# Second layer's output weights loaded from the sync queue, behind the activations of the first two token blocks

## The chip, the cores and the metric

The kernel runs on one core of one Trainium2 chip. The metric is the device time of the whole kernel in microseconds (us); the kernel before is given as the median of three runs, 2333.69 us (2331.33 to 2339.92). The engines are called as in the profile: PE (matrix products and transposes), DVE (VectorE), ACT (ScalarE), POOL (GpSimd) and SP (SyncE, which here only issues transfers).

## The reference

The reference is an encoder of two layers over 1024 tokens of width 1024. The first layer mixes tokens with latent attention, the second with differential attention; both are block-causal over chunks of 64 tokens and have 8 heads. Each layer is

```python
h = _layernorm(ALPHA * h + mix, ln_mix_g[i], ln_mix_b[i])
h = _layernorm(ALPHA * h + _swiglu(h, ffn_w_gu[i], ffn_w_down[i]), ln_ffn_g[i], ln_ffn_b[i])
```

What the change touches is the end of the second layer's mixer, in which the heads' outputs `o`, normalised per head, go through the output weights `w_o` (8 heads of 128 rows by 1024 columns):

```python
o = _rmsnorm(o, g_sub) * (1.0 - lambda_init)
return o.reshape(b, s, DIFF_HEADS * DIFF_V) @ w_o
```

All is float32.

## The kernel before, in words

Products are made in three passes of a reduced format: each operand is split into a high and a low part (`hi`, `lo`), and high by high, high by low and low by high are added up. The split of an activation is one ACT instruction (the high part) and one DVE instruction (the low part). Tokens are worked on in 8 blocks of 128.

*Attention of the second layer* (lines 1190 to 1371) goes over 8 heads and, in each, over the 8 token blocks; `attention` writes the sequence out. For each block PE makes two sets of scores (`s_b`, line 217), DVE adds the bias and finds the row limits (line 220), ACT takes the exponential (line 223), DVE the reciprocal (line 225), POOL scales one of the two maps (line 1269) and DVE adds the two (line 1270). PE then turns the result around (`pt_b`, line 149), ACT and DVE split it (lines 244 and 245), and PE multiplies it with the values (`o_b`, line 256). Scores run two blocks ahead. Other work is put between the blocks by a table of slots, `fill`, with `at(slot, function)`. In the last head the blocks come in the order of `LAST_ORDER`: 6, 7, 4, 5, 2, 3, 0, 1.

*The output product of the second layer* is begun inside the last head. Its class is `OutProj` (line 326). `begin_out` (line 1357), in slot 54, opens it: it frees the layer's input `xT`, which PE reads last in the projections of the last head (`bp`, lines 144 to 146), and in that room asks for the activations and the weights. Heads 0 to 5 (`HEADS = H - 2`) are complete by then and lie in DRAM; `of(tb)` (line 350) loads them for one token block as 128 rows of 6 pieces of 128 numbers (`of_a`, line 355), splits them (`split`, lines 378 and 379), and loads the residual `z` (line 373). The weights of the eight heads lie in DRAM already split (`wo_dr`): heads 0 to 5 come in one load of 1 MB each (`wo`, line 342), heads 6 and 7 in two loads of 0.5 MB each (`who` and `wlo`, line 347). `early` (line 400) multiplies the first two blocks, 6 and 7, with heads 0 to 5 in slots of the last head (`zp_a`, line 390, from `product`); `late` (line 409) adds heads 6 and 7; `rest` (line 417) does the other six blocks and the layer norm, whose scale and shift it loads into `gb` (line 420, 2 x 0.5 MB).

*What sets the order.* Each engine works through its own list of instructions in a fixed order; one that waits holds up all behind it. The order within a list is made when the kernel is built, by a scheduler that follows priorities and an estimate of when each instruction will be ready; a change of one transfer can thus move other instructions too. Issues of transfers stand in the lists of SP and POOL like any other instruction. Each of the two has eight landing signals for its transfers, used in turn, so that an issue also waits for the landing of the one eight before it on that queue.

Of the kernel before, what the change touches and what calls it, by code (L numbers as in the profile page):

```python
# [38 lines left out]
LAST_ORDER = (6, 7, 4, 5, 2, 3, 0, 1)  # L39
# [3 lines left out]
def trunk(  # L43
# [32 lines left out]
    nc = tc.nc  # L76
# [31 lines left out]
    def f32(t):  # L108
        return t.bitcast(F32)
# [216 lines left out]
    class OutProj:  # L326
# [5 lines left out]
        def __init__(self, side, w_dr, o_dram, o_here, x_src, x_dst, scale):  # L332
            self.st = ExitStack()
            self.pool = self.st.enter_context(tc.tile_pool(name="op1", bufs=2, side=side, reuse_waits="tile"))
            self.o_dram, self.o_here, self.x_src, self.x_dst, self.scale = o_dram, o_here, x_src, x_dst, scale
            self.oh, self.z, self.sums, self.m = {}, {}, {}, {}
            self.of(LAST_ORDER[0])
            self.wo = []
            for h in range(H):
                if h < self.HEADS:  # L340
                    t = self.pool.tile([P, 2, D], F32R, tag=f"wo{h}", name=f"wo1_{h}", bufs=1)
                    nc.gpsimd.dma_start(t, w_dr[h])
                    self.wo.append((t[:, 0], t[:, 1]))
                else:
                    t = [wp.tile([P, D], F32R, tag=f"w{p}", name=f"w{p}o1_{h}") for p in "hl"]
                    for p in range(2):
                        nc.gpsimd.dma_start(t[p], w_dr[h][:, p])
                    self.wo.append(t)

        def of(self, tb):  # L350
# [684 lines left out]
    with ast as st:  # L1035
# [106 lines left out]
        def at(slot, fn, *args):  # L1142
            fill.setdefault(slot, []).append(lambda: fn(*args))
# [47 lines left out]
    with ExitStack() as st:  # L1191
# [162 lines left out]
        first, second = LAST_ORDER[:2]  # L1354
# [7 lines left out]
        at(b, begin_out)  # L1362
        for slot, what, args in (
            (2, "early", (first, (0, 1))), (3, "early", (first, (2, 3))), (4, "early", (first, (4, 5))),
            (4, "of", (second,)), (6, "early", (second, (0, 1, 2))), (7, "early", (second, (3, 4, 5))),
            (9, "late", (first,)),
        ):
            at(b + slot, lambda what, *a: getattr(proj[0], what)(*a), what, *args)
# [97 lines left out]
```

## Time and profile before

| | |
|---|---|
| median of three runs | 2333.69 us |
| the three runs | 2331.33, 2339.92, 2333.69 us |
| the profiled execution, first to last instruction | 2331.5 us |
| instructions | 31115 |
| granted PE clock, mean | 0.991 |
| transfers | 288.29 MB, mean 124 GB/s |
| on SP's queue | 96480 packets, 267.48 MB |
| on POOL's queue | 5856 packets, 18.81 MB |

The profile is one execution, and the page gives no other time of it than the span. Times in its rows count from the first instruction. A row of a timeline has start, duration, engine, line of the kernel, operation, `out<-in` by the program's names and the shape; in brackets stand the idle time ahead and what ended it. A name such as `of_a` is the tile without its buffer number, so `of_a` stands for all eight blocks. The durations of matmuls overlap: a row's duration is longer than its step to the next.

### The profile page before, as it was taken

The numbers are of one execution on the slowest core, as the hardware profiler recorded it, in microseconds if no ns is written. First come the engines' busy times: TensorE is split into PE (matmuls) and PEld (weight loads), VectorE is DVE, ScalarE is ACT, GpSimd is POOL, SyncE is SP. The second block draws the span as 40 slices with busy tenths as digits, with TensorE's granted clock in tenths as the row PEclk, the third lists the DMA queues.
The fourth block names the chain that finished last, engine by engine and source line by source line (L and its number), as shares of the span: only waits on it lengthen the run. The fifth ranks groups of instructions, "written<-read, shape, count | busy, mean of one in ns | idle before, by whom it ended". The sixth has DMA issues, their size and how long they took to land. (4 is left out here: it accounts for less than half of the span.)

```text
span 2331.5 us, 31115 instructions
## 1 busy us (share of the span) xinstructions
PE 2254.7 (97%) x11410; PEld 1918.7 (82%) x11410; DVE 1556.9 (67%) x2876; ACT 1017.4 (44%) x2089; POOL 894.8 (38%) x706
## 2 busy tenths in 40 slices
PE   7899999999999999999999999979999999999997
PEld 7898997888888887888888898867788888887885
DVE  4567664596656667677576666666596656658777
ACT  4366664352333333444465656545342333324353
POOL 3233452014444445555432424222014444436564
PEclk9999999999999999999999999989999999999999
DMA  5112324344323238454220212153334323337353
GB/s 201 35 57 89 120 90 161 109 163 153 118 85 131 73 118 320 172 194 153 91 55 19 69 37 69 37 190 101 124 141 151 107 98 106 111 131 303 142 203 118
DMA packets 102490, 288.29 MB, mean 124 GB/s; under 512 B 7856, under 2 KB 30000, under 8 KB 91840
## 3 DMA queue, kind: packets, MB, share of 16 engines
q1 hardware_dynamic: 96480, 267.48, 32.4%
q0 software_dynamic: 5856, 18.81, 2.5%
q8 instruction: 90, 1.47, 0.3%
q14 instruction: 64, 0.52, 0.1%
HBM read 205.00 MB, written 77.07 MB: 121 GB/s over the span
## 5 line engine op out<-in xcount | busy, mean ns | idle before, releaser
L470 ACT CAST op_g<-gr 128x512 fp32r<-128x512 f32 x240 | 147.5, 622 | 410.7 <-PE gb L515 228.1
L471 POOL TENSOR_TENSOR op_g<-gr,op_g 128x512 fp32r<-128x512 f32 x104 | 145.9, 1408 | 303.0 <-DVE tmp L606 153.6
L471 DVE TENSOR_TENSOR op_h<-rh,op_h 128x512 fp32r<-128x512 f32 x154 | 161.4, 1078 | 69.9 <-ACT op_h L470 69.9
L515 PE MATMUL ga<-xh_m,op_g 128*128 128x512 f32 x512 | 168.0, 389 | 0.0
L470 ACT CAST op_h<-rh 128x512 fp32r<-128x512 f32 x154 | 92.9, 619 | 147.7 <-PE dx L783 37.2
L783 PE MATMUL dw<-op_w_t,op_h 128*128 128x512 f32 x660 | 151.4, 390 | 0.2 <-DVE op_h L471 0.2
L783 PEld LDWEIGHTS dw<-op_w_t,op_h 128*128 128x128 f32 x660 | 123.6, 188 | 26.1 <-DVE op_h L471 0.6
L223 ACT ACTIVATE l_b<-l_b,mx_b 128x256 f32<-128x256 f32 (+7 forms) x128 | 99.6, 778 | 76.0 <-DVE mx_b L220 74.3
L1269 POOL TENSOR_SCALAR l_b<-l_b,r_b,cst 128x128 f32<-128x128 f32 (+3 forms) x64 | 52.8, 825 | 204.0 <-DVE r_b L225 194.8
L471 POOL TENSOR_TENSOR op_w_t<-tt,op_w_t 128x512 fp32r<-128x512 f32 x66 | 98.7, 1499 | 78.7 <-ACT op_w_t L470 76.8
L783 PE MATMUL dx<-op_w_b,op_h 128*128 128x512 f32 x528 | 122.6, 391 | 5.9 <-ACT op_w_b L470 3.9
L783 PEld LDWEIGHTS dx<-op_w_b,op_h 128*128 128x128 f32 x528 | 98.4, 188 | 29.8 <-ACT op_w_b L470 4.7
L515 PE MATMUL gb<-t4h_f,op_g 128*128 128x512 f32 x352 | 115.8, 390 | 3.2 <-DVE tmp L598 3.2
L515 PE MATMUL gc<-b22h_f,op_g 128*128 128x512 f32 x352 | 115.6, 389 | 1.0 <-ACT op_g L470 1.0
L471 DVE TENSOR_TENSOR op_g<-gr,op_g 128x512 fp32r<-128x512 f32 x136 | 109.5, 806 | 9.0 <-ACT op_g L470 8.8
L515 PE MATMUL gc<-t1h_f,op_g 128*128 128x512 f32 x352 | 115.5, 389 | 0.0
L515 PE MATMUL gb<-t3h_f,op_g 128*128 128x512 f32 x352 | 115.2, 389 | 0.0
L515 PE MATMUL gb<-t2h_f,op_g 128*128 128x512 f32 x352 | 114.9, 389 | 0.0
L515 PEld LDWEIGHTS ga<-xh_m,op_g 128*128 128x128 f32 x512 | 96.1, 188 | 20.0
L471 POOL TENSOR_TENSOR op_g<-s,op_g 128x512 fp32r<-128x512 f32 x40 | 55.9, 1398 | 142.9 <-ACT op_g L470 142.9
L144 PE MATMUL bp<-xT_f,h_wb 128*128 128x512 f32 x256 | 103.0, 402 | 0.1
L146 PE MATMUL bp<-xT_f,l_wb 128*128 128x512 f32 x256 | 101.6, 397 | 0.0
(381 smaller groups left out, 6788.5 us busy)
## 6 DMA issues: line engine op xcount, KB each, us to landing
gr<-in_w_gu SPq DMA_DIRECT2D x44, 1024.0 KB, 6.6
rh<-h_dr SPq DMA_DIRECT2D x28, 1024.0 KB, 4.9
h_dr<-sh SPq DMA_DIRECT2D x22, 1024.0 KB, 4.9
h_dr<-hp SPq DMA_DIRECT2D x22, 768.0 KB, 4.1
tt<-in_w_dn SPq DMA_DIRECT2D x22, 512.0 KB, 7.6
rh<-h_dr SPq DMA_DIRECT2D x14, 768.0 KB, 4.4
z<-xs_dr SPq DMA_DIRECT2D x16, 512.0 KB, 10.0
rw_b<-in_w_dn SPq DMA_DIRECT2D x8, 1024.0 KB, 8.8
```

The source lines that it names most:

```text
L144: T.matmul(ps_out, lh, rh, start=(i == 0), stop=False)
L146: T.matmul(ps_out, ll, rh, start=False, stop=(i == n - 1))
L223: A.activation(l[:, :n], l[:, :n], AF.Exp, bias=mx, scale=-1.0, accum_out=sm)
L470: A.copy(hi, src)
L471: eng.tensor_tensor(lo, src, f32(hi), ALU.subtract)
L515: T.matmul(o, w[:, a, kc], x[b][:, k, :], start=(first and k == 0 and (a, b) == (0, 0)), stop=(k == 3 and a == 1), skip_group_check=True,)
L783: T.matmul(o, h[:, a, c], w[:, b_], start=(first and (a, b_) == (0, 0)), stop=(last and a == 1), skip_group_check=True,)
L1269: G.tensor_scalar(l1[:, :n], l1[:, :n], r1, nlam, ALU.mult, ALU.mult)
```

## The change

Three things change. The loads of all eight heads' weights are issued by SP instead of POOL; since a transfer from SP does not convert, the destination is written as plain float32 (`f32(t)`). `of` is called for both first blocks, 6 and 7, when the output product is opened, ahead of the weights; before, block 7's call stood in a slot four blocks later. That slot's entry goes.

```diff
-            self.of(LAST_ORDER[0])
+            for tb in LAST_ORDER[:2]:
+                self.of(tb)
             self.wo = []
             for h in range(H):
                 if h < self.HEADS:
                     t = self.pool.tile([P, 2, D], F32R, tag=f"wo{h}", name=f"wo1_{h}", bufs=1)
-                    nc.gpsimd.dma_start(t, w_dr[h])
+                    nc.sync.dma_start(f32(t), w_dr[h])
                     self.wo.append((t[:, 0], t[:, 1]))
                 else:
                     t = [wp.tile([P, D], F32R, tag=f"w{p}", name=f"w{p}o1_{h}") for p in "hl"]
                     for p in range(2):
-                        nc.gpsimd.dma_start(t[p], w_dr[h][:, p])
+                        nc.sync.dma_start(f32(t[p]), w_dr[h][:, p])
...
-            (4, "of", (second,)), (6, "early", (second, (0, 1, 2))), (7, "early", (second, (3, 4, 5))),
+            (6, "early", (second, (0, 1, 2))), (7, "early", (second, (3, 4, 5))),
```

Up to this place in the program all engines' lists are the same. Lines of the changed kernel are one higher from line 338 on.

SP's list at the start of the output product, before: the last attention outputs are stored, `of_a` is loaded block by block (the first number in the name is the block), and `zy_a` is a residual.

```order
L1309 DMA o_dr_3_89<-bo 128x256
L355 DMA of_a_6_15086<-o_dr_3_89 128x6x128
L355 DMA of_a_7_15420<-o_dr_3_89 128x6x128
L355 DMA of_a_4_15742<-o_dr_2_88 128x6x128
L355 DMA of_a_5_15833<-o_dr_2_88 128x6x128
L373 DMA zy_a_4_15747<-xs_dr_99 128x1024
```

The same place in the changed kernel:

```order
L356 DMA of_a_6_15086<-o_dr_3_89 128x6x128
L356 DMA of_a_7_15095<-o_dr_3_89 128x6x128
L343 DMA wo_0_15103<-wo_dr_90 128x2048
L343 DMA wo_1_15105<-wo_dr_91 128x2048
L343 DMA wo_2_15107<-wo_dr_92 128x2048
L343 DMA wo_3_15109<-wo_dr_93 128x2048
L343 DMA wo_4_15111<-wo_dr_94 128x2048
L343 DMA wo_5_15113<-wo_dr_95 128x2048
L348 DMA who_6_15115<-wo_dr_96 128x1024
L348 DMA who_7_15119<-wo_dr_97 128x1024
L348 DMA wlo_6_15116<-wo_dr_96 128x1024
L348 DMA wlo_7_15120<-wo_dr_97 128x1024
```

In both, blocks 6 and 7 come next to each other; the ten weight loads now stand behind them, and blocks 4 and 5 behind those.

POOL's list, which is the other side of it, as a piece of before (`l_b` is the softmax map that POOL scales, with head-local block number; `gb` holds the norm's scale and shift):

```order
L1269 TENSOR_SCALAR l_b_6_1_14865<-l_b_6_1_14865,r_b_6_1_14878,cst 128x896
L342 DMA wo_0_15095<-wo_dr_90 128x2048
L342 DMA wo_1_15097<-wo_dr_91 128x2048
L342 DMA wo_2_15099<-wo_dr_92 128x2048
L342 DMA wo_3_15101<-wo_dr_93 128x2048
L342 DMA wo_4_15103<-wo_dr_94 128x2048
L342 DMA wo_5_15105<-wo_dr_95 128x2048
L420 DMA gb_15679<-in_ln_mix_g 128x1024
L420 DMA gb_15679<-in_ln_mix_b 128x1024
L347 DMA who_6_15107<-wo_dr_96 128x1024
L347 DMA who_7_15111<-wo_dr_97 128x1024
L1269 TENSOR_SCALAR l_b_7_1_14916<-l_b_7_1_14916,r_b_7_1_14929,cst 128x1024
```

and of the changed kernel:

```order
L1270 TENSOR_SCALAR l_b_6_1_14865<-l_b_6_1_14865,r_b_6_1_14878,cst 128x896
L421 DMA gb_15679<-in_ln_mix_g 128x1024
L421 DMA gb_15679<-in_ln_mix_b 128x1024
L1270 TENSOR_SCALAR l_b_7_1_14916<-l_b_7_1_14916,r_b_7_1_14929,cst 128x1024
L1270 TENSOR_SCALAR l_b_6_1_15040<-l_b_6_1_15040,r_b_6_1_15053,cst 128x896
```

The ten weight loads are gone from POOL; the two loads of `gb` stay, and now stand first in its queue.

PE's list where it first uses the weights, before (`s_b_7` are the scores of block 7 in the last head, `zp_a_6` the output product of block 6, its two halves of columns 0 and 1):

```order
L217 MATMUL s_b_6_1_1_15046<-bk_10161,ql_10164 128x448
L390 MATMUL zp_a_6_0_0_15248<-wo_0_15095,oh_a_6_15088 128x512 x2
L390 MATMUL zp_a_6_0_0_15248<-wo_0_15095,ol_a_6_15089 128x512
L390 MATMUL zp_a_6_1_0_15255<-wo_0_15095,oh_a_6_15088 128x512 x2
L390 MATMUL zp_a_6_1_0_15255<-wo_0_15095,ol_a_6_15089 128x512
L217 MATMUL s_b_7_0_0_15116<-bk_10161,bq_10159 128x512
L217 MATMUL s_b_7_0_0_15116<-bk_10161,ql_10164 128x512
L217 MATMUL s_b_7_0_1_15121<-bk_10161,bq_10159 128x512
L217 MATMUL s_b_7_0_1_15121<-bk_10161,ql_10164 128x512
L390 MATMUL zp_a_6_0_0_15248<-wo_1_15097,oh_a_6_15088 128x512 x2
```

and now:

```order
L217 MATMUL s_b_6_1_1_15046<-bk_10161,ql_10164 128x448
L391 MATMUL zp_a_6_0_0_15256<-wo_0_15103,oh_a_6_15088 128x512 x2
L391 MATMUL zp_a_6_1_0_15263<-wo_0_15103,oh_a_6_15088 128x512 x2
L391 MATMUL zp_a_6_0_0_15256<-wo_0_15103,ol_a_6_15089 128x512
L391 MATMUL zp_a_6_1_0_15263<-wo_0_15103,ol_a_6_15089 128x512
L217 MATMUL s_b_7_0_0_15124<-bk_10161,bq_10159 128x512
L217 MATMUL s_b_7_0_0_15124<-bk_10161,ql_10164 128x512
L149 MATMUL pt_b_7_0_15155<-ident,l_b_7_0_14901 128x128 x4
L217 MATMUL s_b_7_0_1_15129<-bk_10161,bq_10159 128x512
L217 MATMUL s_b_7_0_1_15129<-bk_10161,ql_10164 128x512
L256 MATMUL o_b_3_15173<-pth_b_6_0_15062,bvh_0_13904 128x256
L149 MATMUL pt_b_7_1_15164<-ident,l_b_7_0_14901 128x128 x4
```

The first use of the first weight keeps its place behind the same row; the transposes of head 6's last block (`pt_b_7`) now come before the second weight's first use, which follows directly behind this piece.

## The prediction

> **What bounds the kernel now.** The page comes first. It says that TensorE (PE) is the bound of the whole kernel, so that only what PE loses can be won.
>
> ```profile
> span 2331.5 us, 31115 instructions
> PE 2254.7 (97%) x11410; PEld 1918.7 (82%) x11410; DVE 1556.9 (67%) x2876; ACT 1017.4 (44%) x2089; POOL 894.8 (38%) x706
> ```
>
> PE is busy for 2254.7 of 2331.5 us, which leaves 77 us without work. The second view is the list of waits, for PE alone around the moment at which the output weights are fetched (1531 to 1595 us), and then for all engines from 1500 to 1600 us. Columns: who waited, for whom, us in total, times, longest.
>
> ```profile
> PE s_b L217 <- DVE mx_b L220: 14.4, 1, 14.4
> PE zp_a L390 <- DMA wo<-wo_dr: 0.6, 1, 0.6
> ...
> ACT oh_a L378 <- DMA of_a<-o_dr: 15.0, 1, 15.0
> DVE oh_a L379 <- ACT oh_a L378: 13.8, 1, 13.8
> ```
>
> One wait of 14.4 us stands there: nearly a fifth of all that PE loses. Read upward it is a chain. PE waits for VectorE (DVE), DVE for ScalarE (ACT), and ACT for one transfer, the load of attention outputs into `of_a`. The third view, the timeline of PE, shows the place and a second loss behind it. Columns: start, duration, then engine, line and instruction; the bracket is the idle time before it and what ended it.
>
> ```profile
> 1533.16 0.37 PE L217 MATMUL s_b<-bk,ql 128*128 128x448 f32 x1
> 1534.10 0.70 PE L390 MATMUL zp_a<-wo,oh_a 128*128 128x512 f32 x2 [0.57 <-DMA wo<-wo_dr]
> ...
> 1550.59 0.80 PE L217 MATMUL s_b<-bk,bq 128*128 128x512 f32 x1 [14.40 <-DVE mx_b L220]
> ...
> 1555.85 0.39 PE L390 MATMUL zp_a<-wo,oh_a 128*128 128x512 f32 x1
> ...
> 1580.44 2.90 PE L390 MATMUL zp_a<-wo,oh_a 128*128 128x512 f32 x12
> ```
>
> The windows view (busy us of each engine in a stretch, number of instructions, then the granted PE clock, the DMA share and GB/s) gives the clock there.
>
> ```profile
> 1533.50:1536.20 2.70, 2.12 (x9) 1.42 (x8) 0.83 (x3) 0.00 (x0) 0.54 (x1) 1.00 1.04 396
> 1536.20:1550.60 14.40, 0.01 (x1) 0.01 (x1) 2.44 (x7) 2.88 (x6) 2.85 (x4) 0.59 1.07 407
> 1550.60:1555.80 5.20, 5.20 (x12) 4.12 (x13) 3.62 (x11) 2.38 (x4) 1.08 (x1) 0.50 1.13 386
> 1555.80:1589.30 33.50, 33.50 (x207) 29.41 (x205) 24.88 (x76) 20.18 (x53) 7.78 (x8) 1.00 0.05 15
> 1589.30:1600.00 10.70, 8.82 (x37) 6.69 (x36) 9.13 (x28) 7.20 (x20) 1.98 (x3) 0.85 0.39 123
> ```
>
> PE stands still for 14.40 us, and then runs its next 12 matmuls, from 1550.59 to 1555.85, at half the clock: 5.26 us. The 12 alike at 1580.44 take 2.90 us with the tail of the last; the steps are (2.90 - 0.39) / 11 = 0.228 us, so 12 steps are 2.74 us and the slow clock costs 2.52 us. During the standstill the DMA engines are full (share 1.07, 407 GB/s).
>
> Why that one transfer was late is read from the timelines of SyncE (SP), ACT and POOL, and from the list of DMA issues (last column: us from issue to landing), the first and the second issue of the pair apart.
>
> ```profile
> 1527.63 0.96 SPq L355 DMA_DIRECT2D of_a<-o_dr  x2
> ...
> 1547.17 0.93 ACT L378 ACTIVATE oh_a<-of_a,cst 128x768 fp32r<-128x768 f32 x1 [14.98 <-DMA of_a<-o_dr]
> ...
> 1527.91 3.25 POOL L342 DMA_DIRECT2D wo<-wo_dr  x6 [3.77 <-PE bp L146]
> 1531.15 0.54 POOL L420 DMA_DIRECT2D gb<-in_ln_mix_g  x1
> 1531.68 0.54 POOL L420 DMA_DIRECT2D gb<-in_ln_mix_b  x1
> 1537.86 1.19 POOL L1269 TENSOR_SCALAR l_b<-l_b,r_b,cst 128x1024 f32<-128x1024 f32 x1
> ```
>
> ```profile
> of_a<-o_dr SPq DMA_DIRECT2D x1, 384.0 KB, 3.6
> ...
> of_a<-o_dr SPq DMA_DIRECT2D x1, 384.0 KB, 19.1
> ```
>
> SP issues the loads of blocks 6 and 7 within 0.96 us. The first lands after 3.6 us, the second, of the same size and issued at about 1528.1, only after 19.1, at 1547.2. In between, GpSimd (POOL) has issued six weight loads of 1 MB on its own queue. The packets of the two queues, from 1532 to 1546 us (packets, MB, share of 16 engines):
>
> ```profile
> q0 software_dynamic: 733, 5.35, 94.8%
> q1 hardware_dynamic: 733, 0.38, 12.9%
> ```
>
> 733 packets each. The DMA engines take one packet from POOL's queue and one from SP's in turn; the weights have packets of 7.3 KB on average (5.35 MB / 733), `of_a` of 0.5 KB. A load of 384 KB thus waits behind some 6 MB. ACT's order is fixed, with both blocks' conversions ahead of its next softmax work, and so everything stands.
>
> **The change part by part.** The weights now go through SP's queue, behind both loads of `of_a`. What SP's queue does with two transfers in flight, I read at another place, where a store of 768 KB and a load of 1 MB are issued 0.43 us apart:
>
> ```profile
> 591.52 0.37 SPq L631 DMA_DIRECT2D h_dr<-hp  x1
> 591.95 0.48 SPq L524 DMA_DIRECT2D gr<-in_w_gu  x1
> ```
>
> ```profile
> h_dr<-hp SPq DMA_DIRECT2D x1, 768.0 KB, 4.1
> ...
> gr<-in_w_gu SPq DMA_DIRECT2D x1, 1024.0 KB, 6.5
> ```
>
> The first lands at 595.6, the second at 598.4, 2.8 us later, which is the time of 1 MB at 375 GB/s. They were served one after the other. So block 7's load will be through before any weight moves.
>
> *Removed.* The standstill, 14.40 us, and the slow clock behind it, 2.52 us; also the old wait for the first weight, 0.57 us, which is reckoned anew below. Together 17.5 us, all on PE's path. POOL loses ten issues of about 0.54 us (3.25 / 6) and its waits for free places; its softmax scaling, which ran at 1537.86, can then run when its input is there. That is worth nothing more by itself, since all that waited for it was behind the same standstill.
>
> *Added: the wait for the first weight.* PE is ready for it at 1533.16 + 0.37 = 1533.5. Its landing is a sum over SP's queue. Block 6 lands at 1527.63 + 3.6 = 1531.2, as now. Block 7 follows; the rate of such packets, while hardly any weight moved (1529.5 to 1530.5 us), is this:
>
> ```profile
> q1 hardware_dynamic: 611, 0.31, 103.2%
> q0 software_dynamic: 3, 0.02, 6.1%
> ```
>
> 768 packets (384 KB at 0.5 KB) at 611 per us are 1.3 us: 1532.5. Then 1 MB of weight at 409 GB/s (5.35 + 0.38 MB in 14 us), 2.6 us: 1535.1. This is the lower end: a wait of 1.6 us. The upper end comes from what stays on POOL's queue. The two rows of the normalisation's scale and shift (`gb`, 2 x 0.5 MB) stood behind the weights and now stand first. They wait only for PE's last read of the key tile whose place they take:
>
> ```profile
> 1527.79 0.40 PE L217 MATMUL s_b<-bk,ql 128*128 128x512 f32 x1
> ```
>
> That ends at 1528.2, so they are issued near 1528.5. The weights of before, issued at 1527.91, had 3 packets through by 1530.5, some 2.5 us later; `gb` will hence start moving at about 1531, in turn with block 7's small packets, and its 1 MB, 2.6 us, comes in ahead of the first weight: 1537.7, a wait of 4.2 us. I take 4.0, near that end, since it follows from the row of 733 to 733. For block 7 this means a landing of up to 1535.1, 12 us earlier than now; ACT then waits some 3 us for it, under PE's wait.
>
> The next weights follow every 2.6 us. Between the first use and the second PE has, by the new order, six matmuls of weights and four of scores, 10 x 0.228 us, and eight transposes, which take this:
>
> ```profile
> 1557.53 1.03 PE L149 MATMUL pt_b<-ident,l_b 128*128 128x128 f32 x8
> ```
>
> That is 3.3 us, and some 13 us over the four uses after it, counted in the same way, against 4 x 2.6 = 10.4 for the loads. So no second wait: 0, with 1 us as the end on the other side.
>
> *Added: the clock after that wait.* Shorter standstills are on record, with and without a slow clock behind them:
>
> ```profile
> 1597.02 0.66 PE L149 MATMUL pt_b<-ident,l_b 128*128 128x128 f32 x2 [1.54 <-DVE l_b L1270]
> ...
> 1126.10 1.09 PE L149 MATMUL xTp_f<-ident,y_f 128*128 128x128 f32 x8 [2.14 <-DVE y_f L184]
> ```
>
> ```profile
> 1596.80:1600.10 3.30, 3.08 (x9) 2.54 (x10) 2.04 (x7) 1.78 (x5) 0.00 (x0) 0.50 0.00 0
> 1123.00:1128.00 5.00, 2.78 (x20) 2.22 (x19) 3.25 (x6) 1.14 (x3) 2.16 (x4) 1.00 0.23 96
> ```
>
> 1.54 us of idle (among short waits) were followed by 3.3 us at clock 0.50; 2.14 us were not followed by any. At half clock 3.3 us do the work of 1.7, so the price is 0 to 1.7 us. I take 0.9. The Trainium skill, "TensorE: Matmul & The Clock Gate", section "Part 1: The HAM clock gate", says that the clock falls after an idle window of about 3.4 us, and that windows run free; by a whole idle window a wait of 4 us, lying across two, would mostly cost nothing, and the time would be 2320.2. The row of 1.54 us speaks for a lower threshold than a whole window, and the row of 2.14 us against a fixed one.
>
> *Moved.* Behind the weights on SP stand the loads of blocks 4 and 5; ACT's wait for `of_a` has a count of 1, so nobody waited for them, although they too landed behind the weights, and they keep that place. The z load of block 7 keeps its place in SP's order. In the later order PE takes some matmuls of blocks 4 and 5 earlier; as PE loses only 10.70 - 8.82 = 1.9 us from 1589.3 to 1600, I put 0 there, between -1 and +1.
>
> *Sum.* 17.5 - 4.0 - 0.9 = 12.6 us. The profiled execution would go from 2331.5 to 2318.9 us. Its span lies 2.2 us under the median of the three runs (2331.33, 2333.69, 2339.92), so on that scale the forecast is 2333.7 - 12.6 = 2321.1 us. Behind the place PE is the bound, as the 33.50 of 33.50 us after 1555.8 show, and what PE gains there reaches the end. The forecast's own range: 17.5 - 1.6 = 15.9 won at best (2317.8), 17.5 - 4.2 - 1.7 - 1.0 - 1.0 = 9.6 at worst (2324.1).
>
> **The rivals.** *The softmax chain takes the standstill's place (2326).* With PE's stop gone, DVE has 31.8 us of work (0.83 + 2.44 + 3.62 + 24.88) in the stretch from 1533.5 to 1589.3, and 43.2 us for it where it had 55.8. That is 74%, just what it kept up from 1555.8 to 1589.3 (24.88 of 33.50). For this rival: each softmax block goes PE, DVE, ACT, POOL, DVE, PE, with two blocks of lead. Against it: PE has weight matmuls to put between. If DVE reached only 66%, the stretch would be 48 us, 7.6 us won: 2326.
>
> *The queue makes no difference (2333.7).* All transfers still share the same DMA engines and the bytes are the same. If block 7's load is late in SP's queue as it was in two, ACT stops as long, and nothing changes. The Trainium skill, "DMA: Bandwidth & Descriptors", section "Issuing engines are not separate DMA queues", says that transfers of all engines run on the same 16 DMA engines and interleave, and that issuing from several saves only issue time; read strictly it gives this case. The trace agrees on the sharing (733 to 733), but the pair at 591.5 us, one after the other, speaks against the conclusion. That the loads are not reordered at all is excluded by the new order.
>
> *The other side: SP's queue serves what is in flight in turn (2340).* Then block 7's packets alternate with those of six weights and `gb`, and it lands when nearly all is through: 8 MB of weights, 1 MB of `gb` and 0.8 MB of `of_a` from 1529 at 409 GB/s end at 1553, 6 us later than 1547.2, and the first weight as late: about 2333.7 + 6 = 2340. It decides from the point at which block 7 lands after 1547.2. For it: a list of issues shows the order of issue, not of service. Against it: the same pair at 591.5.
>
> **How the numbers follow.** Forecast 0.73, softmax chain 0.13, no difference 0.08, the other side 0.06. A measurement of this kernel can tell about 0.5% from no change, 11.7 us, so the bound lies at 2322.0, inside the forecast's range: I give two thirds of the forecast to the side below, 0.49. Within 0.5% are the rest of the forecast, 0.24, the chain, 0.13, the case of no difference, 0.08, and 0.04 of the other side: 0.49. Slower by more, 0.02. The range takes in the forecast's own and the chain, and the scatter of the three runs (2.4 us below the median, 6.2 above): 2314 to 2330.
>
> **What would show it.** Right: block 7's load lands by 1535.5; the 14.4 us wait of PE is gone; in its place stands one wait for `wo` of 2 to 4 us; `gb` moves between 1531 and 1536; the clock is at 0.50 for 3.4 us at most; from then to the end the rows of both traces run in parallel. Wrong: ACT still waits over 10 us for `of_a`, or PE waits for later weights, or PE collects many waits of about 1 us for DVE, or the place is won and lost again further on.

## The result, and the profile after

The changed kernel takes 2321.85 us (median of four runs, 2316.95 to 2322.50), the kernel before on the same chip 2332.51 us (median of four). The ratio is 0.9948 (95% interval 0.9933 to 0.9963): 10.7 us less between the medians. Here and below a ratio is worked out from the single runs of both kernels, so it need not be the quotient of the two medians.

The page of the changed kernel (the profiled execution is that of 2316.95 us):

```profile
span 2315.2 us, 31103 instructions
PE 2252.5 (97%) x11410; PEld 1917.9 (83%) x11410; DVE 1554.9 (67%) x2876; ACT 1017.8 (44%) x2089; POOL 889.8 (38%) x696
```

PE has the same 11410 matmuls and 2.2 us less of busy time; nearly all that was won is idle time. Its two longest waits in the stretch that answers to the one shown of before (1525 to 1600 us):

```profile
PE zp_a L391 <- DMA wo<-wo_dr: 3.0, 1, 3.0
PE pt_b L149 <- DVE l_b L1271: 2.2, 1, 2.2
...
```

The wait of 14.4 us is gone, and so is ACT's for `of_a`. In its place stands one wait of 3.0 us for the first weight. The second row is a wait that was there before too (1.54 us, at 1597.02 in the prediction's rows). The issues on SP, and the landings:

```profile
1523.87 0.96 SPq L356 DMA_DIRECT2D of_a<-o_dr  x2
1524.88 2.91 SPq L343 DMA_DIRECT2D wo<-wo_dr  x6
```

```profile
of_a<-o_dr SPq DMA_DIRECT2D x1, 384.0 KB, 3.5
...
of_a<-o_dr SPq DMA_DIRECT2D x1, 384.0 KB, 4.2
...
wo<-wo_dr SPq DMA_DIRECT2D x1, 1024.0 KB, 7.8
gb<-in_ln_mix_g POOLq DMA_DIRECT2D x1, 512.0 KB, 7.1
```

Block 7's load, issued at 1524.3, takes 4.2 us in place of 19.1 and lands at 1528.5. The first weight lands at 1524.88 + 7.8 = 1532.7. PE there, and at two later places, first in the changed kernel and then in the kernel before (heads 6 and 7 of the output product; first matmul of the feed-forward part):

```profile
1532.80 2.05 PE L391 MATMUL zp_a<-wo,oh_a 128*128 128x512 f32 x4 [3.03 <-DMA wo<-wo_dr]
...
1573.06 0.40 PE L391 MATMUL zp_a<-who,oh_a 128*128 128x512 f32 x1
...
1662.90 0.48 PE L516 MATMUL ga<-xh_m,op_gp 128*128 128x512 f32 x1
```

```profile
1589.26 0.48 PE L390 MATMUL zp_a<-who,oh_a 128*128 128x512 f32 x1
...
1677.94 0.48 PE L515 MATMUL ga<-xh_m,op_gp 128*128 128x512 f32 x1
```

Count from the issue of block 6's load, 1523.87 now and 1527.63 before. It is 49.2 us to heads 6 and 7 where it was 61.6: **12.4 us won at the place**. To the feed-forward part it is 139.0 where it was 150.3, 11.3 won; to the end of the span 791.3 where it was 803.9, 12.5 won. The spans themselves differ by 16.3; the other 3.8 us arose ahead of the place, where the lists of all engines are the same, and are scatter of one execution.

The clock, by windows (PE's granted clock is the third number from the end):

```profile
1529.80:1530.80 1.00, 0.00 (x0) 0.00 (x0) 1.00 (x2) 0.35 (x2) 0.00 (x0) 1.00 0.99 414
1530.80:1532.80 2.00, 0.00 (x1) 0.03 (x1) 2.00 (x5) 1.00 (x2) 0.00 (x0) 0.51 1.02 412
1532.80:1537.70 4.90, 4.90 (x14) 3.86 (x14) 2.00 (x8) 0.66 (x4) 0.00 (x0) 0.50 1.00 415
1537.70:1573.00 35.30, 35.24 (x209) 30.52 (x208) 26.68 (x77) 21.55 (x55) 9.14 (x9) 1.00 0.44 175
```

It falls one us into the wait and stays at 0.50 until 1537.7, 4.9 us after PE is at work again: 4.9 / 2 = 2.4 us lost. After that PE is busy for 35.24 of 35.30 us.

### The profile page after: what moved, and what is told of

It is laid out like the page before. It is cut to its first block, busy times and chain, and to the rows that moved or that the text cites. A ratio compares the mean times of both kernels' runs of the same rounds, so it can differ in the third digit from the quotient of the medians.

```text
span 2315.2 us, 31103 instructions
## 1 busy us (share of the span) xinstructions
PE 2252.5 (97%) x11410; PEld 1917.9 (83%) x11410; DVE 1554.9 (67%) x2876; ACT 1017.8 (44%) x2089; POOL 889.8 (38%) x696
## 5 line engine op out<-in xcount | busy, mean ns | idle before, releaser
L784 PEld LDWEIGHTS dw<-op_w_t,op_h 128*128 128x128 f32 x660 | 123.5, 188 | 25.9 <-DVE op_h L472 0.4
## 6 DMA issues: line engine op xcount, KB each, us to landing
z<-xs_dr SPq DMA_DIRECT2D x16, 512.0 KB, 10.7
```

The lines of the kernel that those rows point to most:

```text
L784: T.matmul(o, h[:, a, c], w[:, b_], start=(first and (a, b_) == (0, 0)), stop=(last and a == 1), skip_group_check=True,)
```

## The experiments

The theory on trial, from the prediction: block 7's load was late because two queues take turns packet by packet, and ACT, DVE and PE stood behind it. The main rivals: the gain comes from POOL, rid of ten issues; or from having the weights on SP's queue at all, whatever stands where.

| run | ratio to before (95%) | median, us | block 7's load, issue to landing, us | block 6's issue to the feed-forward part, us |
|---|---|---|---|---|
| before | 1 | 2332.51 | 19.1 | 150.3 |
| the change | 0.9948 (0.9933 to 0.9963) | 2321.85 | 4.2 | 139.0 |
| e1, weights on SP alone | 0.9949 (0.9935 to 0.9964) | 2321.84 | 19.6 | 138.3 |
| e2, both loads early alone | 1.0011 (1.0002 to 1.0020) | 2335.88 | 19.5 | 151.5 |
| e7, rows of 3 KB | 0.9947 (0.9930 to 0.9964) | 2322.67 | 4.5 | 135.7 |
| e3, all on POOL | 0.9945 (0.9933 to 0.9957) | 2321.05 | 4.0 | 137.8 |
| e10, weights on ACT | 0.9974 (0.9964 to 0.9984) | 2327.69 | 15.2 | 146.0 |
| e11, conversion late | 0.9962 (0.9950 to 0.9975) | 2325.01 | 20.6 | 139.2 |
| e12, conversion early | 0.9992 (0.9982 to 1.0003) | 2330.79 | 19.6 | 145.2 |
| e4, `gb` on SP | 0.9944 (0.9932 to 0.9957) | 2322.63 | 4.1 | 136.7 |
| e5, first weight between | 0.9939 (0.9927 to 0.9952) | 2321.52 | 9.9 | 141.3 |
| e6, e4 and e5 | 0.9926 (0.9913 to 0.9938) | 2317.57 | 6.2 | 135.7 |
| e13, e6 and rows of 3 KB | 0.9935 (0.9922 to 0.9949) | 2318.34 | 6.4 | 135.8 |

The last two columns are worked out from the timelines and landings of each run's one profiled execution, as above. The experiments ran on three other chips, each beside the kernel before, whose medians there were 2332.91 us (e1, e2, e3, e7), 2335.64 (e4, e5, e6, e10) and 2332.36 (e11, e12, e13). Across chips compare the ratios, not the medians.

### The two halves of the change (e1, e2)

e1 leaves block 7's load in its old slot (against the changed kernel):

```diff
-            for tb in LAST_ORDER[:2]:
-                self.of(tb)
+            self.of(LAST_ORDER[0])
...
-            (6, "early", (second, (0, 1, 2))), (7, "early", (second, (3, 4, 5))),
+            (4, "of", (second,)), (6, "early", (second, (0, 1, 2))), (7, "early", (second, (3, 4, 5))),
```

> Half of the change: weights on SP's queue, but block 7's load of of_a asked for in its old slot, so that on SP it stands behind six weights of 1 MB and two halves of the seventh and eighth. My theory (one queue serves in order, and what counts is that block 7's load stands ahead of the weights): about 7 MB of weights, 1 MB of gb beside them and 0.4 MB of block 6 go first, 8.4 MB at 409 GB/s is 20.5 us, so block 7 lands some 20 to 22 us after block 6's issue, ACT and PE stand as before (14 to 17 us), and the time is 2331 to 2337 us, no better than before. Rival (the gain comes from POOL, rid of ten issues, or from the weights being on SP's queue at all): standstill gone, about 2322.

Measured: all of the gain, against the expectation. The load itself is late, as expected and more; SP's timeline, the landing of the later one, and ACT's timeline in e1:

```profile
1523.44 0.37 SPq L355 DMA_DIRECT2D of_a<-o_dr  x1
1523.86 2.91 SPq L342 DMA_DIRECT2D wo<-wo_dr  x6
...
1529.74 0.37 SPq L355 DMA_DIRECT2D of_a<-o_dr  x1
```

```profile
of_a<-o_dr SPq DMA_DIRECT2D x1, 384.0 KB, 19.6
```

```profile
1527.06 0.94 ACT L378 ACTIVATE oh_a<-of_a,cst 128x768 fp32r<-128x768 f32 x1
...
1532.26 1.04 ACT L223 ACTIVATE l_b<-l_b,mx_b 128x896 f32<-128x896 f32 x1
...
1548.57 0.83 ACT L223 ACTIVATE l_b<-l_b,mx_b 128x640 f32<-128x640 f32 x1
...
1549.91 0.96 ACT L378 ACTIVATE oh_a<-of_a,cst 128x768 fp32r<-128x768 f32 x1
```

The load lands at 1549.3, as late after its issue as before and 25.9 us after block 6's issue (20 to 22 were expected), and nobody waits: block 7's conversion, directly behind block 6's in the kernel before, now stands behind six exponentials in ACT's list. The scheduler, which gives each instruction its place by an estimate of when it is ready, had put it there; that it did so because it reckoned the load as later is likely and not shown. So my expectation, which took ACT's list as it was, was wrong. The new theory is that a standstill needs two things: the load late, *and* its conversion ahead of softmax work. e11 and e12 below try it.

e2 is the other half: the weights back on POOL, both loads asked for together.

```diff
-                    nc.sync.dma_start(f32(t), w_dr[h])
+                    nc.gpsimd.dma_start(t, w_dr[h])
...
-                        nc.sync.dma_start(f32(t[p]), w_dr[h][:, p])
+                        nc.gpsimd.dma_start(t[p], w_dr[h][:, p])
```

> The other half: both loads of of_a asked for together, weights still on POOL's queue. My theory: the two queues still take turns packet by packet, 768 packets of 0.5 KB beside as many of 7.3 KB, so block 7 lands 17 to 20 us after its issue and the time is that of before, 2330 to 2335 us. Rival (asking early is what helps): block 7 lands within 6 us, about 2322. Rival (POOL): as before too, so this run doesn't tell it apart.

```profile
PE s_b L217 <- DVE mx_b L220: 15.2, 1, 15.2
```

The standstill of before, and the load again at 19.5 us. The median, 2335.88 us, is 0.9 us above the range that I had given. This half changes little: the two loads stood next to each other in SP's list before, too, and were issued within 0.96 us. Asking for both together is worth nothing by itself.

### The load's lateness (e7, e3, e10)

e7 is the kernel before with another layout of the attention outputs in DRAM, so that a load of `of_a` reads longer rows:

```diff
-    o_dr = [[dr.tile([H, P, 256], F32, name=f"o_dr{l}_{g}") for g in range(4)] for l in range(2)]
+    o_dr = [[dr.tile([H, P, 256], F32, name=f"o_dr0_{g}") for g in range(4)],
+            [dr.tile([2, P, H, P], F32, name=f"o_dr1_{g}") for g in range(4)]]
...
-            src = self.o_dram[tb // 2][:n, :, (tb % 2) * P:(tb % 2) * P + P]
-            nc.sync.dma_start(of, src.rearrange("h p q -> p h q"))
+            nc.sync.dma_start(of, self.o_dram[tb // 2][tb % 2][:, :n, :])
...
```

The stores, not shown here, write to the same layout.

> The kernel before, with both queues and all slots as they were; only the DRAM tile of attention outputs of layer 2 is laid out so that a load of of_a reads rows of 3 KB in place of 0.5 KB (its stores write rows of 0.5 KB in place of 1 KB). My theory (queues take turns packet by packet): block 7's load has 128 packets in place of 768, is through after as many packets of weights, 128 x (7.3 + 3) KB = 1.3 MB, 3.3 us, and lands 5 to 8 us after its issue in place of 19.1; standstill gone, 2319 to 2325 us. Rival (share by bytes, or by bandwidth): lands as late as before, 2332. Rival (POOL's issues): POOL is as busy as before, 2332.

```profile
of_a<-o_dr SPq DMA_DIRECT2D x1, 384.0 KB, 4.5
```

```profile
1528.30 0.94 ACT L377 ACTIVATE oh_a<-of_a,cst 128x768 fp32r<-128x768 f32 x1
1529.64 0.94 ACT L377 ACTIVATE oh_a<-of_a,cst 128x768 fp32r<-128x768 f32 x1 [0.40 <-DMA of_a<-o_dr]
```

Block 7's conversion still stands directly behind block 6's, and ACT waits 0.40 us for the load where it waited 14.98. So here it is the load that came sooner, and not the reader that moved. The packets of the two queues of e7 from 1527.6 to 1529.6 us, while block 7's load moved beside the weights:

```profile
q0 software_dynamic: 75, 0.61, 78.7%
q1 hardware_dynamic: 85, 0.21, 29.0%
```

Both queues still move nearly as many packets as each other, but the larger packets let the load through at once: 4.5 us in place of 19.1, with the same bytes, queues and slots. PE's wait of 14.4 us for softmax work is gone and the gain is that of the change. That settles that the lateness came from turns by packets, and it excludes POOL, which issues all that it did before, as the source of the gain. The Trainium skill, "DMA: Bandwidth & Descriptors", section "Queues, rings and completion order", says that each DMA engine goes round its queues by packets; the 733 to 733 of before and these rows agree, though they don't show how many packets one turn has. The Trainium skill, "DMA: Bandwidth & Descriptors", section "Issuing engines are not separate DMA queues", says that transfers interleave whichever engine started them, and that starting them on several engines saves only issue time. Here the queue decides more than that: e2 and the changed kernel have both loads in the same order and differ in the weights' queue alone, and block 7's load takes 19.5 us in the one and 4.2 in the other.

e3 puts the two loads on POOL's queue, ahead of the weights that stay there (the weights' lines as in e2):

```diff
-            nc.sync.dma_start(of, src.rearrange("h p q -> p h q"))
             first = tb in LAST_ORDER[:2]
+            (nc.gpsimd if first else nc.sync).dma_start(of, src.rearrange("h p q -> p h q"))
```

> Weights on POOL's queue as before, and the two loads of of_a on POOL's queue as well, ahead of them. My theory (a queue serves in order, whichever engine issues): block 7 lands ahead of the weights, 5 to 9 us after its issue; the standstill of 14.4 us shrinks to a wait of 4 to 8 us for of_a and the first weight, as POOL's packets start about 2.4 us after the issue; 2321 to 2328 us. Rival (POOL must be rid of issues): POOL has two issues more than before, its scaling comes later still, 2332 us or more. Rival (share by bytes): as before.

```profile
of_a<-o_dr POOLq DMA_DIRECT2D x2, 384.0 KB, 4.0
```

The loads land 4.0 us after their issue, sooner than the 5 to 9 expected, and the time is that of the change, with two issues more on POOL than before. It isn't SP's queue, then, nor POOL's relief, but one queue with the load ahead of the weights. e10 has the weights of heads 0 to 5 on a third queue, ACT's, so that POOL is as free as in the change:

```diff
-                    nc.sync.dma_start(f32(t), w_dr[h])
+                    nc.scalar.dma_start(f32(t), w_dr[h])
```

> The changed kernel, with the first six weights issued on ACT's queue in place of SP's, the two loads of of_a staying on SP. So POOL is rid of the issues as in the changed kernel, but weights and of_a are on two queues as before. My theory (queues take turns packet by packet): block 7 lands late again, 12 us or more after its issue, and as ACT now also pays for six issues, PE stands 10 us or more: 2329 to 2336. Rival (POOL rid of its issues is the gain): block 7's lateness does no harm, or doesn't occur, 2322 plus ACT's six issues of 0.5 us, 2322 to 2325.

```profile
PE zp_a L391 <- ACT oh_a L379: 8.9, 1, 8.9
```

```profile
q10 hardware_dynamic: 234, 1.72, 60.5%
q0 software_dynamic: 234, 0.84, 31.9%
q1 hardware_dynamic: 375, 0.19, 9.1%
```

From 1532 to 1539 us the weights (q10) and `gb` (q0) move packet for packet; SP's small ones (q1) bring 0.19 MB. These are 375 to 234, so among three queues the turns aren't one for one, and why stays open. The load takes 15.2 us, and here block 6's is late as well (ACT waits 10.8 us for it), so PE stands 8.9 us, where I had expected 10 or more. The time came out 1.3 us under the range that I had given. POOL is rid of the issues here, and yet only half of the gain is there (0.9974 to 0.9948). Three of ACT's six issues stand behind that wait and come only at 1540; what ACT's issues cost by themselves can't be told apart from the late loads here.

### The place in ACT's list (e11, e12)

These two cross the second condition with the first. e11 is the kernel before, all transfers untouched; block 7's conversion is ordered behind block 4's exponentials, the place it had in e1:

```diff
+    last_exp = {}
...
-        A.activation(l[:, :n], l[:, :n], AF.Exp, bias=mx, scale=-1.0, accum_out=sm)
+        last_exp[name] = A.activation(l[:, :n], l[:, :n], AF.Exp, bias=mx, scale=-1.0, accum_out=sm)
...
-            self.split(tb, slice(0, n), of)
+            if tb == LAST_ORDER[1]:
+                with tc.issue_after(last_exp["b7_4_1"].ins):
+                    self.split(tb, slice(0, n), of)
+            else:
+                self.split(tb, slice(0, n), of)
```

> The kernel before, with all its transfers on their old queues and in their old order; only block 7's conversion on ACT is ordered behind the exponentials of block 4 in the last head, where the run with the weights alone on SP had it by itself. My theory now (the standstill needs two things: block 7's load late, and its conversion ahead of the next softmax work in ACT's list; taking away either is enough): the load still lands 17 to 20 us after its issue, but nobody waits for it there, the standstill of 14.4 us is gone, 2318 to 2325 us, the same as the changed kernel. Rival (the load's lateness itself, or POOL's ten issues, cost the time): 2330 us or more.

```profile
of_a<-o_dr SPq DMA_DIRECT2D x1, 384.0 KB, 20.6
```

```profile
1549.92 0.83 ACT L225 ACTIVATE l_b<-l_b,mx_b 128x640 f32<-128x640 f32 x1 [0.54 <-DVE mx_b L222]
1550.75 0.92 ACT L384 ACTIVATE oh_a<-of_a,cst 128x768 fp32r<-128x768 f32 x1
```

The load is as late as ever (20.6 us, landed at 1545.0), the conversion starts without a wait, the standstill is gone. At the place it gains what the change gains (139.2 to 139.0); its ratio is a little higher, with intervals that overlap, and its median lies at the upper edge of the range expected. e12 is the opposite: e1's transfers, but the exponentials of block 7 may only follow block 7's conversion. Its edit is against the changed kernel:

```diff
+    gate = []
...
-        A.activation(l[:, :n], l[:, :n], AF.Exp, bias=mx, scale=-1.0, accum_out=sm)
+        if name.startswith("b7_7_"):
+            with tc.issue_after(gate[1].ins):
+                A.activation(l[:, :n], l[:, :n], AF.Exp, bias=mx, scale=-1.0, accum_out=sm)
+        else:
+            A.activation(l[:, :n], l[:, :n], AF.Exp, bias=mx, scale=-1.0, accum_out=sm)
...
-            for tb in LAST_ORDER[:2]:
-                self.of(tb)
+            self.of(LAST_ORDER[0])
...
+            self.of(LAST_ORDER[1])
...
-            A.activation(oh, o, AF.Copy, scale=self.scale)
+            gate.append(A.activation(oh, o, AF.Copy, scale=self.scale))
```

> Weights on SP with block 7's load behind eight of them, as in the run with the weights alone on SP, but the exponentials of block 7 in the last head are ordered behind block 7's conversion in ACT's list. My theory: the load lands 24 to 27 us after block 6's issue, ACT stops for it for some 10 us, and PE, which has weights' products to put between, stands 4 to 12 us: 2325 to 2334 us. Rival (having the weights on SP's queue is enough by itself): 2322.

```profile
PE zp_a L397 <- ACT oh_a L385: 2.9, 1, 2.9
PE zp_a L397 <- DMA wo<-wo_dr: 2.5, 3, 1.6
PE o_b L262 <- ACT pth_b L250: 2.1, 1, 2.1
PE o_b L262 <- DVE ptl_b L251: 1.3, 1, 1.3
...
ACT oh_a L385 <- DMA of_a<-o_dr: 4.5, 1, 4.5
```

ACT waits for the load (4.5 us, less than the 10 expected), PE collects waits behind it, and no gain is left in the time that can be measured (0.9992, with 1 inside the interval), though the weights are on SP's queue and POOL is rid of them. In the profiled execution 5.1 us are still won at the place (145.2 against 150.3, with e1 at 138.3), so the conversion's place undoes somewhat more than half of the gain there. That speaks against the rivals which credit SP's queue or POOL's relief, and completes the square: load late with the conversion high in the list is slow (before, e2, e12); load soon (the change, e3, e7) or conversion low (e1, e11) is fast.

### What is left of the first weight's wait (e4, e5, e6, e13)

e4 moves `gb` to SP, behind the weights; e5 issues the first weight between the two loads; e6 does both; e13 adds e7's layout.

```diff
-                nc.gpsimd.dma_start(gb[:, i], src.partition_broadcast(P))
+                nc.sync.dma_start(gb[:, i], src.partition_broadcast(P))
```

```diff
-            for tb in LAST_ORDER[:2]:
-                self.of(tb)
+            self.of(LAST_ORDER[0])
             self.wo = []
             for h in range(H):
+                if h == 1:
+                    self.of(LAST_ORDER[1])
```

> The changed kernel, with the two loads of gb on SP behind the weights. My theory (the wait for the first weight is stretched by gb, whose 1 MB moves in turn with it): wo_0 lands some 2.4 us earlier, 6 to 6.8 us after block 6's issue in place of 8.8, PE's wait for it goes from 3.0 to 0.5 us or less, the clock of 0.50 behind it (2.3 us lost) goes too: 4 to 5 us won, 2317 to 2318 us. Rival (the wait is block 7's load and the first 1 MB themselves): wait stays near 3, 2321 to 2322.

```profile
PE zp_a L391 <- DMA wo<-wo_dr: 1.2, 1, 1.2
```

```profile
1535.50:1538.90 3.40, 3.35 (x10) 2.64 (x11) 3.40 (x11) 1.40 (x3) 0.00 (x0) 0.59 1.01 429
```

The wait falls to 1.2 us, not to 0.5, and 3.4 us at a clock of 0.59 follow it still. At the place 2.4 us are won in the profiled execution (136.7 against 139.0), but from there to the end it takes longer, and the time is that of the change: 4 to 5 us were expected, and none can be measured. A part of what was given back shows in the last feed-forward part, where PE waits for `z`, first the change and then e4:

```profile
PE dw L784 <- DVE z L800: 2.8, 2, 1.5
```

```profile
PE dw L784 <- DVE z L800: 4.7, 2, 3.2
```

> The changed kernel, with the first weight's load between those of block 6 and block 7. My theory (gb takes its turn with whatever stands first): block 7's 0.4 MB, 1.3 us, goes out of the first weight's way, its wait falls from 3.0 to 1.0 to 1.7 us; block 7 lands 3 to 5 us later, at which ACT waits a little under PE's work; 0 to 3 us won by the clock behind, 2319 to 2322. Rival (block 7's load is the critical one here too): its lateness of 4 us shows at PE as a wait for DVE, 2322 to 2326.

```profile
PE o_b L256 <- ACT pth_b L244: 3.0, 1, 3.0
PE zp_a L392 <- DMA wo<-wo_dr: 0.8, 1, 0.8
```

The wait for the weight falls to 0.8 us, and a wait of 3.0 us for ACT, which waits 5.7 us for block 7's load (9.9 us), takes its place. The mechanism is the rival's; the time, 2321.52 us, is that of the change.

> Both: first weight between the two loads of of_a, and gb on SP behind the weights. My theory: the first weight lands before PE is ready, no wait for it; block 7 lands 2.6 us later than with gb alone moved, still within 8 us of block 6's issue; 4 to 6 us won against the changed kernel, 2316 to 2318. Rival: block 7 late, a wait of PE for DVE in place of that for the weight, 2320 or more.

```profile
PE zp_a L392 <- DMA wo<-wo_dr: 0.5, 2, 0.3
```

Only 0.5 us of waiting for weights are left. e6 has the lowest median, 2317.57 us, and the lowest ratio, 0.9926 against 0.9948 of the change; the intervals overlap a little (0.9913 to 0.9938, 0.9933 to 0.9963), so that it is better than the change is likely and not shown.

> Candidate: the changed kernel with the first weight between the two loads of of_a, gb on SP behind the weights, and of_a in rows of 3 KB. By my theory each load of of_a is through in about 1 us in place of 1.3 (384 KB at 409 GB/s), so block 7 and the second weight come some 0.5 us earlier than with 0.5 KB rows; that is less than the scatter: 2315 to 2319 us, the same as without the layout within the error. A gain of more than 3 us would say that small packets still cost in one queue.

2318.34 us and 135.8 us at the place, as e6: small rows cost nothing more that can be measured once the load shares no queue turn with the weights.

## Why the prediction was right

*Removed, 17.5 us: right.* The standstill, its slow clock and the old wait for the weight are all gone. e7, e11 and e12 show the chain that the prediction read out of the waits.

*The wait for the first weight, 4.0 taken: 3.0.* The step that was mis-sized is that all of `gb` comes in ahead of the weight, in turn with block 7's small packets. `gb` began to move only between 1527.5 and 1528.0, when block 7's load was nearly through. By the landing of that load, at 1528.5, 0.19 MB of `gb` were in; after that the turns were with the weight. The two queues of the changed kernel from 1528.5 to 1532.7:

```profile
q1 hardware_dynamic: 156, 1.15, 66.3%
q0 software_dynamic: 155, 0.57, 33.1%
```

Packet for packet once more, but the weight's packets are twice as large (7.4 KB to 3.7). So 0.57 MB of `gb` came in beside the weight, and with the 0.19 MB before them 0.76 MB in place of all of its 1 MB.

*The clock, 0.9 taken, 1.7 at most: 2.4.* The bound was wrong. It came from one stretch of 3.3 us at half clock; after this wait half clock held for 4.9 us of PE's work. The nearer row was the one behind the 14.40 us, where half clock held for 5.2 us. The sign that was named for it, at most 3.4 us at 0.50, did not come either.

*Later weights, 0: right.* No second wait for `wo` stands in the list. *The later order, 0: right within its bounds.* With the measured sizes the sum is 17.5 - 3.0 - 2.4 = 12.1, and 12.4 were won at the place. Two errors, of 1.0 us and of 1.5 us, nearly cancelled, and that the 12.6 taken came so close is in part luck.

*What is won reaches the end: right.* 12.5 us to the end of the span. The medians differ by less, 10.7; the interval of the ratio is 8.6 to 15.6 us of 2332.51, and both lie in it.

*Block 7's load is through before any weight moves: right*, by 4.2 us after its issue, and e1 shows it from the other side, as a load that stood behind the weights in the same queue came after them. *POOL's relief is worth nothing by itself: right as far as shown*; e3, e7 and e11 gain with POOL as busy as before, and e12, with POOL rid of the issues, has no gain in the time that can be measured.

*The rivals.* Of the softmax chain next to nothing shows: behind 1537.7 PE loses 0.06 of 35.30 us, and the later wait for DVE, 1.5 us before, is 2.2. That the queue makes no difference, and that one queue serves in turn, both fall with the 4.2 us.

*What the prediction left out.* It named ACT's fixed order as a link and then took it as given. It is half of the cause. Moving the weights to SP alone gives the whole gain (e1), because the conversion then stands lower in ACT's list; that the scheduler put it there for reckoning the load as late is likely and not shown. "Both asked for together" adds nothing to that which can be measured (0.9948 against 0.9949).

## What to carry to other kernels

A late transfer costs only as much as the order of the engine that reads it lets it: before moving transfers, look whether its reader can stand lower in its list. Where a small-row load and a large-row one are in flight on two queues, the small one gets a share by packets, not by bytes; put it on the same queue ahead, or make its rows longer. And try the parts of a change one by one, since with a scheduler one part may bring all of it by another road.

## What the runs showed of the hardware

The clock doesn't go by the length of a single wait. In the changed kernel it fell one us into a wait of 3.0 us (1.00 to 1530.8, 0.51 behind it), though PE had been busy for 4.33 of the 4.77 us ahead of the wait; in e4 a wait of 1.2 us was followed by 0.59; in e1 this wait of 1.6 us, ahead of 1533.6, by none:

```profile
1532.00:1533.60 1.60, 0.01 (x1) 0.02 (x1) 0.80 (x4) 1.60 (x4) 0.00 (x0) 1.00 1.05 438
1533.60:1537.00 3.40, 3.40 (x20) 3.01 (x21) 1.88 (x6) 0.89 (x3) 0.00 (x0) 1.00 1.02 404
```

The Trainium skill, "TensorE: Matmul & The Clock Gate", section "Part 1: The HAM clock gate", has the clock fall after an idle window of some 3.4 us; a fall after one us of idle time disagrees with a whole window of it. What the clock counts stays open. And a queue with longer rows changes the outcome as much as a change of queue: 19.1 us to 4.5 for the same 384 KB (e7).
